# A two-sequence encoder layer: norms of the next sequence, operands of the MLP's first group and the filling at the ends of branch B put in another order

## The chip, the cores and the metric

The kernel runs on one core of a Trainium2 chip. The metric is the device time of one launch, in microseconds (us); lower is better. Engines are named as the profile does: PE (matrix multiply), DVE (vector), ACT (scalar, activation), POOL (general), SP (here it only issues DMAs).

## The reference

One layer of an encoder, all in float32, over two inputs with the same weights: `x_sample` (1 x 512 x 1024) and `x_prompt` (1 x 1024 x 1024).

```python
D_MODEL, HEAD_DIM, D_FF, GRID_W = 1024, 64, 4096, 64

def _token_mixer(xn, w_in, ...):
    z = xn @ w_in
    qa, ka, va, qb, kb, vb, ga, gb = jnp.split(z, idx, axis=-1)
    ...
    o_a = _gqa_attention(qa, ka, va)            # 8 heads, 2 key/value heads
    o_b = _neighbourhood_attention(qb, kb, vb, rpb)   # 8 heads, window 8 x 16 on the token grid
    merged = jax.nn.sigmoid(ga) * (o_a @ w_proj_a) + jax.nn.sigmoid(gb) * (o_b @ w_proj_b)
    return merged @ w_out

def _trunk(x, ...):
    h = x + _token_mixer(_rmsnorm(x, norm_mix_g[l]), ...)
    hn = _rmsnorm(h, norm_mlp_g[l])
    h = h + jnp.square(jax.nn.relu(hn @ w_mlp_up[l])) @ w_mlp_down[l]
    return _rmsnorm(h, norm_final_g)
```

## The kernel before

Every matrix product of float32 operands is made of three passes: each operand is cut into a high part (`hi`, written by ACT, L180 or L1253) and a remainder (`lo`, by DVE, L186 or L1254), and `mm3` (L190) issues hi x hi, lo x hi and hi x lo, which the profile shows as L191, L192 and L193. So each operand of PE passes over ACT and then DVE, and mostly comes from a DMA that SP issues.

The token mixer runs twice (`run`, a "trunk" each), first over `x_sample` (512 tokens, `NB` = 1 block of 512) and then over `x_prompt` (1024 tokens, `NB` = 2). A trunk has these stretches: norm and transposes of x into `xs` (`norm_tile` L249, `transpose_tile` L271, whose PSUM tile is `ptx`), the projection `zs`, branch A, branch B and the merge with the output projection ("phase G"). The MLP then runs over all 1536 tokens in two blocks of 768.

**Branch B** goes through units of one head and one group of 128-query blocks: n = 16 units in the first sequence, 32 in the second. A unit passes three steps, each one unit behind the one before: scores on PE (`sbs`, L930, from `kBs` and `qBs`) with the exponentials, transposes of the probabilities (`ptbs`, L955 and L961, copied to `bhs`), and the product with the values (`obs`, L987). The result of the two last heads goes ACT (`ot_B`), DVE (`os_B`, L994), POOL (L1007), ACT (L1014) and DVE (L1015) into `oX3`, the last of the four operands of the merge. Between the steps PE is given other products, "filling": generators in `fill`, of which `fill.pull(k)` takes k pieces (a piece is one `mm3` of 512 columns). Near the end the filling is `proj_a`, which computes `o_a @ w_proj_a` (`ppas`, 32 pieces in the first sequence), and before it the gate products (`gpss`). How many pieces a unit gets is the number `f` (L1031 to L1034). `proj_a` loads the last part of branch A's output (`rawos`, split into `oXs`) when it is started.

**Phase G** computes `o_b @ w_proj_b` per 128 output columns c (`ppbs`, four `mm3` each, k = 0 to 3, the last from `oX3`), merges, and then computes `merged @ w_out` in two halves of the columns, tile by tile of 128 tokens (`ops`, 24 matmuls each). In the second half of the first sequence, per tile, it also loads a tile of the next sequence's x (`xas`), norms it (`xnns`) and transposes it (`ptxs`), and norms its own output for the MLP (`xnhs`). Loads of the next sequence's first weights (`rawqs`, `rawkvs`, `raw_vs`) come from the pool `rawp`, which has three buffers of 512 KB, tag "raw".

**The MLP** multiplies 2 x 2 blocks with seven products in place of eight. The seven right operands `B_0` to `B_6` are made of transposed tiles by `pair_t` (L310): b11, b21, b12, b22 are four PSUM banks of transposes (`pt`), a1 to a4 sums of them. `pair_t` is called in phase G of the second sequence for three pairs of tiles. The seven left operands `A_0` to `A_6` of a group of 256 columns of `w_mlp_up` are made by `up_steps`, sums `S_0` to `S_3` first where one is needed; the group before carries these steps as "side steps". `up` issues the products into the banks `ua` to `ud`: 12 matmuls of 384 columns each.

The order on each engine is not that of the program text: a scheduler in the build orders all instructions from the data dependences and its own costs, apart from those that `keep_in_program_order` (or `pin=True`) holds in place. Each engine works through its own queue in order.

Of the kernel before, what the change touches and what calls it, by code (L numbers as in the profile page):

```python
# [18 lines left out]
P = 128  # L19
# [42 lines left out]
def encoder(ctx: ExitStack, tc: tile.TileContext, xs, outs, w):  # L62
# [247 lines left out]
    def pair_t(nm, j, tiles, B, banks, tmp):  # L310
# [23 lines left out]
        nc.vector.tensor_tensor(a1, y1, b11, op=ALU.subtract)  # L334
        nc.vector.tensor_tensor(a2, b22, a1, op=ALU.subtract)
        hi(1, a2)
        hi(2, a1)
        nc.vector.tensor_tensor(a3, b22, y1, op=ALU.subtract)
        hi(3, a3)
        nc.vector.tensor_tensor(a4, b21, a2, op=ALU.subtract)  # L340
        hi(4, b22)
        hi(5, b21)
        hi(6, a4)
        lo(4, b22)
        lo(5, b21)
        lo(1, a2)
        lo(2, a1, nc.gpsimd)
        lo(3, a3)
        lo(6, a4, nc.gpsimd)
# [45 lines left out]
    def run(tr, nxt, first):  # L395
# [428 lines left out]
        with phase(f"phB{N}") as ph:  # L824
# [205 lines left out]
            for i in range(n + LS + LV):  # L1030
                if NB == 1:  # L1031
                    f = 9 if i < 1 else 5 if i < n - 4 else 7
                else:
                    f = 5 + (i % 3 > 0) if i < n - 8 else 7  # L1034
# [21 lines left out]
                if i == n - (6 if first else 8):  # L1056
                    pa = proj_a(ph)
                    next(pa)
# [13 lines left out]
        with phase(f"phG{N}") as ph:  # L1072
# [25 lines left out]
            for c in range(NC8):  # L1098
                wp = wp_b.pop(0)
                for c_ in {0: (1, 2), NC8 - 2: (), NC8 - 1: ()}.get(c, (c + 2,)):  # L1100
                    wp_b.append(load_cols(w["w_proj_b"][0], c_ * P, P, f"pb{N}_{c_}", pool_wp))
                for tb in range(NB):
# [5 lines left out]
                    sg = tmp_zs(f"zs{nm}")  # L1108
                    nc.sync.dma_start(sg, zg[1][c * P : (c + 1) * P, tb * 512 : tb * 512 + 512])
                    p_ = mm(f"ppb{nm}")  # L1110
                    for k in range(4):
                        mv = [
                            oX[k][:, i, :].rearrange("p (j r c) -> p r j c", j=4, c=16)[:, tb * 8 : tb * 8 + 8, :, :]
                            for i in range(2)
                        ]
                        mm3(p_, wp[k][0], wp[k][1], mv[0], mv[1], k == 0, k == 3)
# [19 lines left out]
            ahead = []  # L1136

            for half in range(2):
                wo = wos[half]
                hc = slice(half * 512, half * 512 + 512)  # L1140
                for tt in range(NT):
# [15 lines left out]
                    if half == 1 and nxt is not None:  # L1157
                        xt = ph.tile([P, D], F32, tag="k4", name=f"xa{nm}", bufs=4)
                        nc.sync.dma_start(xt, nxt.x[tt * P : (tt + 1) * P, :])
                        ahead.append((tt, norm_tile(xt, gn, ph, f"n{nm}", "k4", 4)))  # L1160
# [68 lines left out]
    def mlp():  # L1229
# [68 lines left out]
        def up_steps(st, ops):  # L1298
# [26 lines left out]
            return [lambda i=i: one(i) for i in (0, 1, 2, 3, 4, 6, 5)]  # L1325
# [7 lines left out]
        def up(st, A, B, side):  # L1333
# [32 lines left out]
            def put(f, half, src, in1=None):  # L1366
# [9 lines left out]
                if f == 0:  # L1376
# [15 lines left out]
            prod(a, 5, 5, True)  # L1392
            put(0, 0, a)
# [108 lines left out]
        def run_up(b, A, B, last):  # L1502

            for fb in range(NFB):
# [5 lines left out]
                up((b, fb), A, B, spread(side, 7))  # L1510
# [265 lines left out]
```

## Time and profile before

| | |
|---|---|
| time, median of 3 runs | 2152.71 us (2152.17 to 2154.12) |
| the profiled execution, own time | 2152.51 us |
| its span in the profile | 2150.7 us |
| granted PE clock, mean | 0.997 |
| DVE, ACT, POOL busy | 69%, 52%, 18% |
| HBM | 264.85 MB read, 87.88 MB written, 164 GB/s over the span |

Places in the span: branch B of the first sequence ends near 310 us and that of the second near 1060; the second half of phase G of the first sequence lies from 356 to 382; the three `pair_t` of phase G from 1184 to 1209; the MLP begins near 1210.

How to read a row of the timeline: start, duration, engine, line, operation, output<-input with shapes, count; in brackets the engine's idle time ahead of the row and what released it. PE's matmuls overlap, so the distance between two starts is what one costs, not its duration. Rows that stand in the prediction aren't shown here.

### The profile page before, as it was taken

Reading aid. Unit: us, or ns where it says so; the run is one execution under the profiler, and the core shown is the slowest. Engines: PE = TensorE matmul, PEld = TensorE weight load, DVE = VectorE, ACT = ScalarE, POOL = GpSimd, SP = SyncE. Lnnn points to the kernel's source line nnn. Section 1 sums busy time; section 2 is a strip of 40 time slices with the busy share of each in tenths; the row PEclk is TensorE's granted clock in tenths of the full one; section 3 lists DMA queues with packets and bytes.
Section 4 is the critical chain, followed back from the end, with each engine's and each line's share of the span. In section 5 each row is a group of like instructions: output and inputs, shape, how many; then the busy total and the mean of one; then the engine's idle time right before and its main releaser. Section 6 shows DMA issues by size and latency. Waiting matters only on the chain. (4 is left out here: it accounts for less than half of the span.)

```text
span 2150.7 us, 31785 instructions
## 1 busy us (share of the span) xinstructions
PE 2120.9 (99%) x10970; PEld 1849.3 (86%) x10970; DVE 1476.2 (69%) x2801; ACT 1115.5 (52%) x2343; POOL 395.3 (18%) x506
## 2 busy tenths in 40 slices
PE   9999999999999999999999999999999999999998
PEld 8887878888898888887888899999999988888886
DVE  6675686677657754656781877778777777759563
ACT  5665554556636644555540566566655643434352
POOL 2232420432243214433300200003000000000000
PEclk9999999999999999999999999999999999999999
DMA  6435557520122132433462655568444799688561
GB/s 195 127 106 163 166 171 256 171 75 25 49 79 75 43 98 86 125 107 102 146 222 106 213 191 180 184 233 222 149 156 154 250 354 338 217 273 282 174 201 63
DMA packets 319578, 350.91 MB, mean 163 GB/s; under 512 B 31160, under 2 KB 255032, under 8 KB 319417
## 3 DMA queue, kind: packets, MB, share of 16 engines
q1 hardware_dynamic: 277927, 279.65, 41.2%
q10 hardware_dynamic: 35810, 52.19, 7.0%
q0 software_dynamic: 5680, 17.04, 2.8%
q8 instruction: 87, 1.43, 0.3%
q14 instruction: 74, 0.61, 0.1%
HBM read 264.85 MB, written 87.88 MB: 164 GB/s over the span
## 5 line engine op out<-in xcount | busy, mean ns | idle before, releaser
L193 PE MATMUL dn<-wd,al 128*128 128x512 f32 x624 | 242.8, 389 | 0.0
L192 PE MATMUL dn<-wd,ah 128*128 128x512 f32 x624 | 242.8, 389 | 0.0
L191 PE MATMUL dn<-wd,ah 128*128 128x512 f32 x624 | 242.7, 389 | 0.0
L1253 ACT ACTIVATE ah<-ar 128x512 fp32r<-128x512 f32 x168 | 104.2, 628 | 199.8 <-PE dn L192 188.6
L1254 DVE TENSOR_TENSOR al<-ar,ah 128x512 fp32r<-128x512 f32 x168 | 115.8, 696 | 76.9 <-ACT ah L1253 65.7
L191 PEld LDWEIGHTS dn<-wd,ah 128*128 128x128 f32 x624 | 117.1, 188 | 24.4
L192 PEld LDWEIGHTS dn<-wd,ah 128*128 128x128 f32 x624 | 117.1, 188 | 24.3
L193 PEld LDWEIGHTS dn<-wd,al 128*128 128x128 f32 x624 | 117.1, 188 | 24.2
L724 POOL TENSOR_SCALAR ps<-ps,rls 128x1024 f32<-128x1024 f32 (+1 forms) x96 | 96.8, 1010 | 215.5 <-DVE rls L723 202.6
L764 DVE TENSOR_TENSOR ptls<-pTs,pths 128x512 fp32r<-128x512 f32 x160 | 107.7, 687 | 37.9 <-ACT pths L763 37.1
L763 ACT ACTIVATE pths<-pTs 128x512 fp32r<-128x512 f32 x160 | 94.2, 598 | 73.8 <-PE pTs L758 71.4
L718 DVE TENSOR_REDUCE nms<-ss 128x1 f32<-128x1024 f32 (+1 forms) x96 | 99.9, 1041 | 25.4 <-PE ss L716 24.9
L176 POOL TENSOR_TENSOR rs_f<-ms_f,mhalf 128x1 f32<-128x1 f32 x6 | 4.0, 667 | 590.7 <-DVE ms_f L172 590.7
L721 ACT ACTIVATE ps<-ss,nms 128x1024 f32<-128x1024 f32 (+1 forms) x96 | 93.3, 973 | 22.5 <-DVE nms L718 20.0
L191 PE MATMUL gpss<-xs_0h,w_gs 128*128 128x512 f32 x256 | 104.7, 409 | 0.3
L758 PEld LDWEIGHTS pTs<-ident,ps 128*128 128x128 f32 x640 | 78.1, 140 | 28.2 <-POOL ps L724 4.3
L193 PE MATMUL gpss<-xs_0h,w_gs 128*128 128x512 f32 x256 | 100.9, 394 | 0.0
L192 PE MATMUL gpss<-xs_0l,w_gs 128*128 128x512 f32 x256 | 100.8, 394 | 0.0
L758 PE MATMUL pTs<-ident,ps 128*128 128x128 f32 x640 | 98.9, 274 | 1.3 <-DVE ptls L764 0.6
L1253 ACT ACTIVATE A<-S 128x512 fp32r<-128x512 f32 x128 | 75.9, 623 | 30.8 <-DVE S L1316 23.5
L1254 DVE TENSOR_TENSOR A<-S,A 128x512 fp32r<-128x512 f32 x128 | 84.5, 686 | 3.9 <-ACT A L1253 3.9
L191 PE MATMUL ud<-B,A 128*128 128x384 f32 x256 | 85.7, 335 | 1.5 <-DVE c L1371 1.5
(325 smaller groups left out, 6380.0 us busy)
## 6 DMA issues: line engine op xcount, KB each, us to landing
ar<-ud SPq DMA_DIRECT2D x120, 512.0 KB
br<-in_w_mlp_down_dram SPq DMA_DIRECT2D x72, 512.0 KB
rawu<-in_w_mlp_up_dram SPq DMA_DIRECT2D x64, 512.0 KB
ud<-c ACTq DMA_DIRECT2D x128, 192.0 KB
raw_gs<-in_w_in_dram SPq DMA_DIRECT2D x32, 512.0 KB
zgs<-sgs ACTq DMA_DIRECT2D x48, 256.0 KB
ud<-cs SPq DMA_DIRECT2D x64, 192.0 KB
raw_os<-in_w_out_dram SPq DMA_DIRECT2D x16, 512.0 KB
```

The lines of the kernel that those rows point to most:

```text
L176: nc.gpsimd.tensor_tensor(r[:, :n], m[:, :n], mhalf[:, :n], op=ALU.pow)
L191: nc.tensor.matmul(out, ah, bh, start=start, stop=False, **kw)
L192: nc.tensor.matmul(out, ah, bl, start=False, stop=False, **kw)
L193: nc.tensor.matmul(out, al, bh, start=False, stop=stop, **kw)
L718: nc.vector.tensor_reduce(nm_, s, axis=AX.X, op=ALU.max, negate=True)
L721: nc.scalar.activation(p, s, AF.Exp, bias=nm_, accum_out=l)
L724: nc.gpsimd.tensor_scalar(p, p, rl, 1.0, op0=ALU.mult, op1=ALU.mult)
L758: nc.tensor.transpose(pt[:, j * P : (j + 1) * P], PP[u, j][:, kc * P : (kc + 1) * P], ident)
L763: nc.scalar.activation(hi, pt, AF.Copy)
L764: nc.vector.tensor_tensor(lo, pt, hi.bitcast(F32), op=ALU.subtract)
L1253: nc.scalar.activation(hi, src, AF.Copy)
L1254: nc.vector.tensor_tensor(lo, src, hi.bitcast(F32), op=ALU.subtract)
```

## The change

Five orders are changed; PE computes the same products.

1. `pair_t`: `B_4`'s high part is copied earlier, and the low parts that read PSUM (`B_4`, `B_5`) come ahead of those that read sums (`B_1`, `B_3`); POOL's two low parts are asked for earlier.
2. Filling of branch B: in the first sequence, the last four units get 6 pieces in place of 7, and the two steps after the last unit 4 and 2. In the second sequence `proj_a` starts a unit earlier (n-9) and the unit n-10 gets no filling.
3. Phase G, c = 0, second sequence: the two products with k = 3 come after the six others.
4. Second half of phase G, first sequence: the four `xas` loads are issued at the first tile, two of them into `rawp`; a tile's norm is issued one tile ahead and its steps, like the `hs` sums, are held in order.
5. MLP, first group of the first block: `A_5`, which is no sum, is made first, and its product is the second, in a bank of its own (`ue`), added to `ua` on DVE.

```diff
@@ -332,21 +332,21 @@
         nc.scalar.activation(y1, b12, AF.Copy)
         lo(0, b11)
         nc.vector.tensor_tensor(a1, y1, b11, op=ALU.subtract)
+        hi(4, b22)
+        hi(2, a1)
         nc.vector.tensor_tensor(a2, b22, a1, op=ALU.subtract)
-        hi(1, a2)
-        hi(2, a1)
+        lo(2, a1, nc.gpsimd)
+        nc.vector.tensor_tensor(a4, b21, a2, op=ALU.subtract)
+        hi(5, b21)
         nc.vector.tensor_tensor(a3, b22, y1, op=ALU.subtract)
-        hi(3, a3)
-        nc.vector.tensor_tensor(a4, b21, a2, op=ALU.subtract)
-        hi(4, b22)
-        hi(5, b21)
         hi(6, a4)
         lo(4, b22)
+        lo(6, a4, nc.gpsimd)
         lo(5, b21)
+        hi(1, a2)
+        hi(3, a3)
         lo(1, a2)
-        lo(2, a1, nc.gpsimd)
         lo(3, a3)
-        lo(6, a4, nc.gpsimd)
...
@@ filling of branch B @@
-                    f = 9 if i < 1 else 5 if i < n - 4 else 7
+                    f = 9 if i < 1 else 5 if i < n - 4 else 6 if i < n else 4 if i == n else 2
                 else:
-                    f = 5 + (i % 3 > 0) if i < n - 8 else 7
+                    f = 0 if i == n - 10 else 5 + (i % 3 > 0) if i < n - 8 else 7
...
-                if i == n - (6 if first else 8):
+                if i == n - (6 if first else 9):
                     pa = proj_a(ph)
...
@@ phase G @@
+                todo = [(tb, k) for tb in range(NB) for k in range(4)]
+                if c == 0:
+                    todo.sort(key=lambda e: e[1] == 3)
+                for tb, k in todo:
...
@@ second half of phase G @@
-                    if half == 1 and nxt is not None:
-                        xt = ph.tile([P, D], F32, tag="k4", name=f"xa{nm}", bufs=4)
-                        nc.sync.dma_start(xt, nxt.x[tt * P : (tt + 1) * P, :])
-                        ahead.append((tt, norm_tile(xt, gn, ph, f"n{nm}", "k4", 4)))
+                    if half == 1 and nxt is not None and tt == 0:
+                        for t_ in (0, 1, 2, 3):
+                            if t_ < 2:
+                                xa[t_] = ph.tile([P, D], F32, tag="k4", name=f"xa{N}_{t_}", bufs=4)
+                            else:
+                                xa[t_] = rawp.tile([P, D], F32, tag="raw", name=f"xa{N}_{t_}")
+                            nc.sync.dma_start(xa[t_], nxt.x[t_ * P : (t_ + 1) * P, :])
+                        ahead.append((0, norm_tile(xa[0], gn, ph, f"n{N}_0", "k4", 4)))
...
-                    while ahead:
+                    if half == 1 and nxt is not None and tt + 1 < NT:
+                        ahead.append((tt + 1, norm_tile(xa[tt + 1], gn, ph, f"n{N}_{tt + 1}", "k4", 4, True)))
+                    if half == 1 and ahead:
                         nxt.p0_t(*ahead.pop(0))
                     if ht is not None:
-                        nc.vector.tensor_tensor(ht[:, hc], o, xr, op=ALU.add)
+                        op = nc.vector.tensor_tensor(ht[:, hc], o, xr, op=ALU.add)
+                        if half == 1 and nxt is not None:
+                            tc.keep_in_program_order(op)
...
@@ MLP @@
-            return [lambda i=i: one(i) for i in (0, 1, 2, 3, 4, 6, 5)]
+            return [lambda i=i: one(i) for i in ((0, 5, 1, 2, 3, 4, 6) if st == (0, 0) else (0, 1, 2, 3, 4, 6, 5))]
...
             prod(a, 0, 0, False)
             nc.scalar.activation(s1, a, AF.Copy)
+            if st == (0, 0):
+                e = bank(f"ue{nm}")[:, 0:HB]
+                prod(e, 5, 5, False)
+                put(0, 0, e, s1)
             prod(bk, 1, 1, False)
...
-            prod(a, 5, 5, True)
-            put(0, 0, a)
+            if st != (0, 0):
+                prod(a, 5, 5, True)
+                put(0, 0, a)
...
-                up((b, fb), A, B, spread(side, 7))
+                if (b, fb) == (0, 0):
+                    side = [[], []] + spread(side, 5)
+                else:
+                    side = spread(side, 7)
+                up((b, fb), A, B, side)
```

What stands on PE at the end of branch B of the first sequence, before (`ppas_7_0` is the last filling, `obs_7_1` and `obs_7_0` the last two units of head 7, `ppbs_0_0` the first merge product, `oXs_1_k` its operand k):

```order
L191 MATMUL ppas_7_0_3735<-oXs_0_3_3251,w_pas_7_3689 128x512
L192 MATMUL ppas_7_0_3735<-oXs_0_3_3251,w_pas_7_3689 128x512
L193 MATMUL ppas_7_0_3735<-oXs_0_3_3251,w_pas_7_3689 128x512
L987 MATMUL obs_7_1_3751<-bhs_7_1_3669,vss_7_3402 128x256 x4
L987 MATMUL obs_7_0_3763<-bhs_7_0_3721,vss_7_3402 128x256 x4
L191 MATMUL ppbs_0_0_3813<-oXs_1_0_3781,w_pbs_0_3731 128x512
L192 MATMUL ppbs_0_0_3813<-oXs_1_0_3781,w_pbs_0_3731 128x512
```

and now:

```order
L193 MATMUL ppas_6_0_3713<-oXs_0_2_3245,w_pas_6_3667 128x512
L987 MATMUL obs_7_0_3737<-bhs_7_0_3695,vss_7_3402 128x256 x4
L191 MATMUL ppas_6_0_3713<-oXs_0_3_3251,w_pas_6_3667 128x512
L192 MATMUL ppas_6_0_3713<-oXs_0_3_3251,w_pas_6_3667 128x512
L193 MATMUL ppas_6_0_3713<-oXs_0_3_3251,w_pas_6_3667 128x512
L191 MATMUL ppas_7_0_3759<-oXs_0_0_3233,w_pas_7_3709 128x512
L192 MATMUL ppas_7_0_3759<-oXs_0_0_3233,w_pas_7_3709 128x512
...
L191 MATMUL ppas_7_0_3759<-oXs_0_3_3251,w_pas_7_3709 128x512
L192 MATMUL ppas_7_0_3759<-oXs_0_3_3251,w_pas_7_3709 128x512
L193 MATMUL ppas_7_0_3759<-oXs_0_3_3251,w_pas_7_3709 128x512
L191 MATMUL ppbs_0_0_3813<-oXs_1_0_3781,w_pbs_0_3755 128x512
L192 MATMUL ppbs_0_0_3813<-oXs_1_0_3781,w_pbs_0_3755 128x512
```

The two `obs` no longer stand together: six `ppas` matmuls are between them, and fifteen between the last `obs` and the first `ppbs` (the first five and the last three of them are shown).

SP's queue in the second half of phase G of the first sequence, before (`xas_1_t` is the next sequence's tile t, `xrs_1_t` a tile of this sequence's x, `raw_os` weights of the output projection, the other `raw` tiles the next sequence's first weights):

```order
L1159 DMA xas_1_0_4161<-in_x_prompt_dram 128x1024
L1152 DMA xrs_1_1_4224<-in_x_sample_dram 128x512
L216 DMA raw_os_1_6_4145<-in_w_out_dram 128x2x512
L448 DMA rawqs_0_0_4425<-in_w_in_dram 128x4x256
L1152 DMA xrs_1_2_4285<-in_x_sample_dram 128x512
L1152 DMA xrs_1_3_4346<-in_x_sample_dram 128x512
L448 DMA rawqs_0_1_4429<-in_w_in_dram 128x4x256
L463 DMA rawkvs_0_4437<-in_w_in_dram 128x8x64 x2
L1159 DMA xas_1_1_4226<-in_x_prompt_dram 128x1024
L216 DMA raw_vs_0_0_4446<-in_w_in_dram 128x4x256
L216 DMA raw_vs_0_4_4451<-in_w_in_dram 128x4x256
L1159 DMA xas_1_2_4287<-in_x_prompt_dram 128x1024
```

and now (`xas_t` is tile t):

```order
L1170 DMA xas_0_4161<-in_x_prompt_dram 128x1024
L1170 DMA xas_1_4163<-in_x_prompt_dram 128x1024
L216 DMA raw_os_1_6_4145<-in_w_out_dram 128x2x512
L1159 DMA xrs_1_1_4238<-in_x_sample_dram 128x512
L1170 DMA xas_2_4165<-in_x_prompt_dram 128x1024
L1159 DMA xrs_1_2_4297<-in_x_sample_dram 128x512
L1159 DMA xrs_1_3_4356<-in_x_sample_dram 128x512
L1170 DMA xas_3_4167<-in_x_prompt_dram 128x1024
L448 DMA rawqs_0_0_4425<-in_w_in_dram 128x4x256
L448 DMA rawqs_0_1_4429<-in_w_in_dram 128x4x256
L463 DMA rawkvs_0_4437<-in_w_in_dram 128x8x64 x2
L216 DMA raw_vs_0_0_4446<-in_w_in_dram 128x4x256
```

`xas_1`, which stood behind five weight loads, now directly follows `xas_0`, and `xas_2` and `xas_3` stand ahead of all weights of the next sequence. On PE the transposes `ptxs_1`, `ptxs_2` and `ptxs_3` stand now after the products of tiles 1, 2 and 3, and before stood near the ends of tile 2, tile 3 and inside the first `zs`.

ACT at the beginning of the MLP, before (`A_0_i` is left operand i of the first group, `A_1_i` of the second, `s_0_0` the two copies of a product bank that later sums need; each `A` row is followed on DVE by its remainder):

```order
L1253 ACTIVATE A_0_1_13126<-S_0_0_13128 128x512
L1253 ACTIVATE A_0_2_13135<-S_0_0_13127 128x512
L1253 ACTIVATE A_0_3_13138<-S_0_0_13129 128x512
L1253 ACTIVATE A_0_4_13142<-S_0_0_13130 128x512
L1253 ACTIVATE A_0_6_13146<-rawu_0_1_13120 128x512
L1253 ACTIVATE A_0_5_13149<-rawu_0_1_13120 128x512
L1253 ACTIVATE A_1_0_13175<-rawu_1_0_13122 128x512
L1380 ACTIVATE s_0_0_13160<-ua_0_13156 128x384
L1384 ACTIVATE s_0_0_13161<-uc_0_13158 128x384
L1253 ACTIVATE A_1_1_13191<-S_0_1_13193 128x512
```

and now:

```order
L1268 ACTIVATE A_0_5_13126<-rawu_0_1_13120 128x512
L1268 ACTIVATE A_0_1_13129<-S_0_0_13131 128x512
L1268 ACTIVATE A_0_2_13138<-S_0_0_13130 128x512
L1268 ACTIVATE A_0_3_13141<-S_0_0_13132 128x512
L1268 ACTIVATE A_0_4_13145<-S_0_0_13133 128x512
L1268 ACTIVATE A_0_6_13149<-rawu_0_1_13120 128x512
L1395 ACTIVATE s_0_0_13160<-ua_0_13156 128x384
L1268 ACTIVATE A_1_0_13206<-rawu_1_0_13122 128x512
L1387 ACTIVATE c_0_0_13189<-c_0_0_13189 128x384
L1388 ACTIVATE c_0_0_13189<-c_0_0_13189 128x384
L1389 DMA ud_0_0_13090<-c_0_0_13189 128x384
```

`A_0_5` moved from sixth to first, and `A_1_0`, an operand of the next group, from ahead of the copy `s_0_0` to behind it. On PE the product of `A_0_5` stands second, and the first twelve matmuls of the next group (`ua_1`) are spread between the last three products of the first.

More of the change, by code (lines that the diff above doesn't have):

```diff
@@ L1101, in run @@
                     wp_b.append(load_cols(w["w_proj_b"][0], c_ * P, P, f"pb{N}_{c_}", pool_wp))
+                zs_of, pp_of = {}, {}
                 for tb in range(NB):
@@ L1107, in run @@
                     nm = f"{N}_{c}_{tb}"
[L1108 to L1116, printed above, removed]
+                    zs_of[tb] = tmp_zs(f"zs{nm}")
+                    nc.sync.dma_start(zs_of[tb], zg[1][c * P : (c + 1) * P, tb * 512 : tb * 512 + 512])
+                    pp_of[tb] = mm(f"ppb{nm}")
+                todo = [(tb, k) for tb in range(NB) for k in range(4)]
+                if c == 0:
+                    todo.sort(key=lambda e: e[1] == 3)
+                for tb, k in todo:
+                    mv = [
+                        oX[k][:, i, :].rearrange("p (j r c) -> p r j c", j=4, c=16)[:, tb * 8 : tb * 8 + 8, :, :]
+                        for i in range(2)
+                    ]
+                    mm3(pp_of[tb], wp[k][0], wp[k][1], mv[0], mv[1], k == 0, k == 3)
+                    if k < 3:
+                        continue
+                    sg, p_ = zs_of[tb], pp_of[tb]
                     nc.vector.scalar_tensor_tensor(sg, sg, 1.0, p_, op0=ALU.add, op1=ALU.mult)
@@ L1135, in run @@
                 gn = gn[:, 0]
-            ahead = []
+            ahead, xa = [], {}
             for half in range(2):
@@ L1375, in put @@
                 kept[f, half] = t
-                if f == 0:
+                if (1 - f, half) in kept:
                     late.append(lambda: total(half))
```

## The prediction

> **What bounds the kernel now.** I read the page's first part, then PE's list of waits, then the timeline of all engines at each wait.
>
> ```profile
> span 2150.7 us, 31785 instructions
> PE 2120.9 (99%) x10970; PEld 1849.3 (86%) x10970; DVE 1476.2 (69%) x2801; ACT 1115.5 (52%) x2343; POOL 395.3 (18%) x506
> ```
>
> PE is busy 2120.9 of 2150.7 us. The change takes no matmul away, so it can win only from the 29.8 us in which PE stands and from stretches in which it runs slowly. The list of PE's waits says which of that the change can reach:
>
> ```profile
> PE ptxs L275 <- DVE xnns L259: 3.0, 3, 2.2
> PE ppbs L191 <- ACT oXs L1014: 2.1, 2, 1.8
> PE ud L191 <- DVE c L1371: 1.5, 1, 1.5
> PE ppas L192 <- DVE oXs L186: 1.2, 1, 1.2
> PE sbs L930 <- DVE kBs L892: 0.8, 1, 0.8
> PE pt L315 <- DVE B L327: 0.8, 1, 0.8
> PE ub L191 <- ACT A L1253: 0.7, 1, 0.7
> ```
>
> Columns: total, times, longest. The seven rows hold 10.1 us, and each one lies where an edit falls. Two of the waits cost more than they last, which the windows show (PE's busy time, then the granted clock, then the DMA share):
>
> ```profile
> 313.50:316.90 3.40, 3.40 (x9) 0.50 0.52 169
> ...
> 388.60:392.00 3.40, 3.40 (x13) 0.50 1.00 337
> ```
>
> About a microsecond after each of the two longest waits (they end at 312.50 and 387.40, in the rows of parts 1 and 3) the clock is 0.50 for 3.4 us. So I count three sorts of loss: the gap, the slow matmul behind it, and the half clock.
>
> **Part 1, filling kept for the end of branch B, first sequence.** All engines there, then PE's next matmuls:
>
> ```profile
> 309.66 0.59 ACT L992 ACTIVATE ot_Bs<-obs 64x512 f32<-64x512 f32 x1 [0.81 <-DVE os_Bs L994]
> 310.12 0.39 PE L192 MATMUL ppbs<-oXs,w_pbs 128*128 128x512 f32 x1
> 310.28 0.68 DVE L994 TENSOR_TENSOR os_Bs<-obs,ot_Bs 64x512 f32<-64x512 f32 x1 [0.72 <-ACT ot_Bs L992]
> 310.34 0.39 PE L193 MATMUL ppbs<-oXs,w_pbs 128*128 128x512 f32 x1
> 311.05 0.96 POOL L1007 TENSOR_TENSOR os_Bs<-os_Bs 64x256 f32<-64x256 f32 x1 [0.61 <-DVE os_Bs L994]
> 312.04 0.41 ACT L1014 ACTIVATE oXs<-os_Bs 64x256 fp32r<-64x256 f32 x1 [1.15 <-POOL os_Bs L1007]
> 312.50 0.50 PE L191 MATMUL ppbs<-oXs,w_pbs 128*128 128x512 f32 x1 [1.77 <-ACT oXs L1014]
> ...
> 313.98 0.63 PE L192 MATMUL ppbs<-oXs,w_pbs 128*128 128x512 f32 x1
> 314.40 0.63 PE L193 MATMUL ppbs<-oXs,w_pbs 128*128 128x512 f32 x1
> ```
>
> Matmuls of 512 columns start 0.23 us apart (310.12, 310.34) and 0.42 us apart at half clock (313.98, 314.40). From 310.34 to 312.50 are 2.16 us, 1.93 over the step. The next two steps are some 0.3 over. In 3.4 us of half clock eight matmuls pass that need 8 x 0.23 = 1.84, so 1.5 are lost. Together **3.7 us**. The chain is ACT, DVE, POOL, ACT: from 309.66 to 312.50, 2.84 us. What covers it after the last `obs` is nine `ppbs` products, 9 x 0.23 = 2.1 us, and the two last `obs` stand side by side, so that ACT's second copy waits 0.81 us for the first one's DVE step. After the change fifteen `ppas` matmuls stand ahead of the nine: 24 x 0.23 = 5.5 us against a chain of 2.9 (4.0 if the 0.81 and a slow POOL step stay). I take 0 left, so gain 3.7. Its price: the units before have six or fewer fill products between them where there were seven, 0.7 us less cover each. The steps before a unit's transposes take 2 to 3 us by these durations, and the shortest new interval is 3.2 us. Bounds: 2 (half the gap comes back upstream, no half clock) to 3.7.
>
> **Part 2, the same in the second sequence.** There one `proj_a` starts a unit earlier, one unit gets no fill, and the last `rawos` is split earlier:
>
> ```profile
> 1005.44 1.38 DVE L892 TENSOR_TENSOR kBs<-pkbs,kBs 64x512 fp32r<-64x512 f32 x2 [0.75 <-ACT kBs L890]
> ...
> 1013.11 1.05 ACT L180 ACTIVATE oXs<-rawos 128x1024 fp32r<-128x1024 f32 x1
> 1014.19 2.60 DVE L186 TENSOR_TENSOR oXs<-rawos,oXs 128x512 fp32r<-128x512 f32 x2 [0.16 <-ACT oXs L180]
> ```
>
> `oXs` at 1014.19 is read at once by `ppas`: the 1.2 us wait of the list, 1.37 with the slow matmul. One of its two DVE steps took 1.9 us, since 0.69 is the step's usual time (1.38 for two). Split a unit earlier, it is off the path: 0. The eight `gpss` matmuls (8 x 0.23 = 1.8 us) now stand between the last `pkbs` and its `sbs`, where PE waited 0.8 (0.95 with the step). But `kBs` now stands behind the two `oXs` steps on DVE (1.38 us), so I leave 0.3. Gain 0.65 + 1.37 = **2.0**; bounds 0 (the two DVE steps are slow there as well, 2.6) to 2.3. Part 2b, `ppbs` with both last thirds at the end: the second `ppbs` wait in the list, 2.1 - 1.8 = 0.3, with its slow matmul **0.5**; nine more matmuls (2 us) cover it.
>
> **Part 3, norms one tile further ahead.**
>
> ```profile
> 349.81 2.96 ACT L180 ACTIVATE wh_os<-raw_os 128x1024 fp32r<-128x1024 f32 x3 [1.50 <-DMA raw_os<-in_w_out_dram]
> ...
> 356.51 0.73 PE L275 MATMUL ptxs<-ident,xnns 128*128 128x128 f32 x5
> ...
> 371.00 0.45 SPq L1159 DMA_DIRECT2D xas<-in_x_prompt_dram  x1
> ...
> 377.22 1.06 ACT L253 ACTIVATE xnns<-xas 128x1024 f32<-128x1024 f32 x1 [1.89 <-DMA xas<-in_x_prompt_dram]
> ...
> 380.16 0.34 SPq L1159 DMA_DIRECT2D xas<-in_x_prompt_dram  x1
> 383.94 1.06 ACT L253 ACTIVATE xnns<-xas 128x1024 f32<-128x1024 f32 x1 [4.53 <-DMA xas<-in_x_prompt_dram]
> 384.70 0.33 PE L191 MATMUL zs<-wghs,xs_0h 128*128 128x384 f32 x1
> 384.87 0.34 PE L192 MATMUL zs<-wgls,xs_0h 128*128 128x384 f32 x1
> 385.97 1.28 DVE L259 SCALAR_TENSOR_TENSOR xnns<-xas,rs_ns,gns 128x1024 f32<-128x1024 f32 x1 [0.69 <-POOL rs_ns L176]
> 387.40 1.06 PE L275 MATMUL ptxs<-ident,xnns 128*128 128x128 f32 x8 [2.19 <-DVE xnns L259]
> 389.33 0.52 PE L191 MATMUL zs<-wghs,xs_0h 128*128 128x384 f32 x1
> 389.65 0.52 PE L192 MATMUL zs<-wgls,xs_0h 128*128 128x384 f32 x1
> ```
>
> The load issued at 380.16 lands at 383.94; the norm then takes 3.3 us (383.94 to 387.25), and PE waits. The three waits are 3.0 us by the list, 3.5 with the slow matmuls behind them. At half clock a 384-column matmul takes 0.32 in place of 0.17: ten in 3.4 us, so 1.5 lost. Together 5.0. Afterwards all four loads are issued in tile 0, and a norm has one tile's 24 matmuls and eight transposes, 24 x 0.23 + 0.9 = 6.4 us, against its 3.3 and what is ahead of it on ACT and DVE (`xs` copies and an `xnhs` norm, up to 3). By this sum the second norm comes about 2 us early and the last one about on time. I leave 0.5: gain **4.5**; bounds 1 (the last one waits over 1.5 us and half clock follows) and 5. What is moved with it: two of the loads now sit in the `raw` buffers, so `rawkvs` of the next sequence waits for the norm of tile 2 and goes out near 372.6, not before 360, and the second `rawqs` some 10 us later. That is the second rival. On SP's queue a second 512 KB load now stands ahead of the last `raw_os`. Before, ACT had split that one by 352.8, and tile 0 (begun just ahead of its transposes at 356.51) reads it after 18 matmuls, so near 361: 8 us of slack, cost 0. The `hs` sums held in order are read by no PE step: 0.
>
> [...]
>
> **Part 4, the MLP's first blocks.**
>
> ```profile
> 1190.43 2.38 DVE L327 TENSOR_TENSOR B<-ta,B 128x512 fp32r<-128x512 f32 x2
> 1192.74 1.27 DVE L327 TENSOR_TENSOR B<-pt,B 128x512 fp32r<-128x512 f32 x2
> ...
> 1213.03 2.20 ACT L1253 ACTIVATE A<-S 128x512 fp32r<-128x512 f32 x4 [5.40 <-PE ua L193]
> 1216.57 1.68 ACT L1253 ACTIVATE A<-rawu 128x512 fp32r<-128x512 f32 x3 [1.35 <-issue]
> ...
> 1223.72 0.55 DVE L1371 TENSOR_TENSOR c<-ud,s 128x384 f32<-128x384 f32 x1
> ```
>
> `pair_t`: the second pair's transposes waited 0.8 for DVE's last read of PSUM, which stood behind two steps on SBUF (2.38 us, one of them 1.7). Ahead of them it ends 2.4 us earlier: **0.9** with the slow matmul, all of it. `ub` waited 0.7 (with what follows 1.3) for the first sum on ACT at 1213.03; a product of twelve 384-column matmuls, 12 x 0.174 = 2.1 us, whose operand is no sum, now stands ahead: **1.3**. `ud` waited 1.5 (1.6) for `c`, which waits for a copy on ACT behind three `A` at 1216.57 to 1218.15. The copy comes 0.5 to 1 us sooner after the last of fewer `A`, and ten matmuls of the next group (1.7 us) are put in between, but the order 2, 3, 4, 6 leaves `uc` and `ud` as close as before to `s` and `c`, and DVE has one more sum (0.55). I leave 0.9: gain **0.7**. Bounds of the three: 1.5 to 3.8. In the MLP's second block `pair_t` is reordered too; PE's list names no wait there, and other products stand between its transposes: 0.
>
> **Sum.** 3.7 + 2.0 + 0.5 + 4.5 + 0.9 + 1.3 + 0.7 = 13.6. For waits that show up nearby and that I can't name I take off 1: of the parts, the second and third are nearest to one. Against the profiled execution, 2152.51 us (span 2150.7 and 1.8 around it, 0.2 under the median of 2152.71): 2152.5 - 12.6 = **2140**.
>
> **The rivals.**
> 1. Part of it comes back: the last norm and the next sequence's weights are late, `kBs` and `uc` wait again. The lower bounds are 2 + 0 + 0.5 + 1 + 1.5 = 5, so 2147.5; typical 2145. For it: part 3 has no margin at its last norm. Against: each place has 2 to 3 us of new cover.
> 2. Slower than before: `rawkvs`, issued near 372.6, must land and be split before `zs` at about 381.7. Loads here took 6.2 us (371.00 to 377.22) and 3.8 us to their first reader, and the split takes under 2: done near 380.6 at the latest, a margin of 1. It turns into a wait from a landing of 7.3 us on, and half clock behind it costs 1.5. To be slower by 0.2% it must take all 12.6 and 4.3 more, so a landing 15 us later: 2157. The DMA share of 1.00 at 388.60 shows that queues can be full.
> 3. No change: the waits move but sum up the same, as PE's list would show under other names: 2151. Or the gaps don't set the clock and the half clock stays: 2140 + 3 = 2143. Against it: both stretches follow the two longest waits. [...]
>
> **How the numbers follow.** All parts within their values, 2136.5 to 2143: 0.52. Rival 1, 2143 to 2148: 0.26. Half clock stays, near 2143: 0.05. No change by 0.2%, which is 4.3 us, about what a measurement can tell here: 0.13. Rival 2: 0.04. Faster 0.83, same 0.13, slower 0.04. Low end: all bounds at their best, 3.7 + 2.3 + 0.5 + 5 + 3.8 = 15.3, so 2137, and 1 for small waits elsewhere: 2136. High end 2148, leaving 0.17 out.
>
> **What would show it.** PE's list without `ppbs` from `oXs`, `ptxs` from `xnns`, `ppas` from `oXs` and `pt` from `B`; clock 1.00 in the windows near 313 and 388; `ud` and `sbs` with under 1 us each. Wrong if a new row above 1 us stands there: `zs` waiting for `wghs` above all, `ptbs` in the units before the end of branch B, or a half-clock stretch elsewhere.

## The result and the profile after

| | us |
|---|---|
| before, median of 6 runs | 2153.56 (2152.17 to 2154.4) |
| changed, median of 6 runs | 2143.10 (2142.86 to 2143.44) |
| ratio | 0.9952, 95% interval 0.9939 to 0.9965 |
| profiled execution, before and after | 2152.51 and 2143.44 |

The change gains 10.5 us by the medians and 9.1 by the two profiled executions, where 12.6 were forecast (2140; the range 2136 to 2148 holds the time). The profile's first part after:

```profile
span 2141.7 us, 31786 instructions
PE 2116.6 (99%) x10970; PEld 1848.3 (86%) x10970; DVE 1469.3 (69%) x2802; ACT 1115.4 (52%) x2343; POOL 393.4 (18%) x506
```

PE stood 29.8 us before and stands 25.1 now. Of its busy time 4.3 us went as well; the two half-clock stretches of before, which the profile after doesn't have, are about 3 of them by the prediction's 1.5 each, and the rest isn't broken down here. PE's list of waits after (total, times, longest):

```profile
PE zs L193 <- DVE xs_1l L291: 2.5, 2, 1.5
...
PE pqs L568 <- DVE rrs L679: 1.2, 1, 1.2
PE sbs L930 <- DVE kBs L892: 1.1, 2, 0.7
...
PE ptxs L275 <- DVE hs L1199: 0.6, 1, 0.6
...
PE ppas L191 <- DVE kBs L892: 0.4, 1, 0.4
...
PE ptbs L955 <- POOL pbs L940: 0.4, 1, 0.4
...
PE uc L191 <- ACT s L1403: 0.2, 1, 0.2
```

The first of these rows in the list of before:

```profile
PE zs L193 <- DVE xs_1l L291: 0.5, 1, 0.5
```

`ppbs` from `oXs`, `ptxs` from `xnns`, `ppas` from `oXs`, `pt`, `ub` and `ud` are gone, all that the change aimed at but one: `sbs` waits for `kBs` still. The wait of `zs` for `xs_1l` grew from 0.5 to 2.5 us and that of `pqs` for `rrs` is new, 3.2 us more in two rows that the prediction had no term for. By stages, first before, then after (window, its length, PE's busy time, granted clock, DMA share; length less busy is PE's idle time; the stages end at other times after the change, so the windows do too, and before the change PE has no idle time from 350 to 365 us):

```profile
300.00:317.00 17.00, 15.23 (x67) 0.90 0.59 186
365.00:393.00 28.00, 25.01 (x123) 0.94 0.81 273
393.00:440.00 47.00, 45.08 (x308) 1.00 0.34 107
1000.00:1030.00 30.00, 27.95 (x137) 1.00 0.45 137
1185.00:1230.00 45.00, 41.95 (x220) 1.00 0.65 213
```

```profile
300.00:317.00 17.00, 17.00 (x83) 1.00 0.71 207
350.00:390.00 40.00, 39.39 (x203) 1.00 0.69 224
390.00:436.00 46.00, 41.66 (x287) 1.00 0.41 126
995.00:1026.00 31.00, 29.42 (x149) 1.00 0.58 176
1180.00:1226.00 46.00, 45.68 (x246) 1.00 0.68 219
```

| stage | PE idle before | after | part |
|---|---|---|---|
| end of branch B, first sequence | 1.8, clock 0.90 | 0 | 1 |
| norms ahead | 3.0, clock 0.94 | 0.6 | 3 |
| first projections of the second sequence | 1.9 | 4.3 | none |
| end of branch B, second sequence | 2.0 | 1.6 | 2 |
| pair_t and first MLP group | 3.0 | 0.3 | 4 |

Two rows differ from the forecast: the projections (row 3) lose 2.4 us more, and the end of the second branch B (row 4) wins 0.5 in place of 2.0. The experiments ask why.

### The profile page after: what moved, and what is told of

Same layout as the page of the kernel before. It is cut to its first block, busy times and chain, and to the rows that moved or that the text cites. A ratio compares the mean times of both kernels' runs of the same rounds, so it can differ in the third digit from the quotient of the medians.

```text
span 2141.7 us, 31786 instructions
## 1 busy us (share of the span) xinstructions
PE 2116.6 (99%) x10970; PEld 1848.3 (86%) x10970; DVE 1469.3 (69%) x2802; ACT 1115.4 (52%) x2343; POOL 393.4 (18%) x506
## 4 chain that ended last, share of the span: by engine, by line
PE 50%; DVE 1%; issue 0%; ACT 0%; DMA 0%; POOL 0%; POOLq 0%; DVEq 0%; ACTq 0%
PE dn L191 6%; PE dn L193 6%; PE dn L192 6%; PE uc L191 2%; PE ud L192 2%; PE uc L192 2%; PE ud L191 2%; PE ud L193 2%; PE uc L193 2%; PE ua L193 2%; PE ua L192 2%; PE ua L191 2%; PE ops L191 1%; PE ops L192 1%; PE ops L193 1%; PE ub L192 1%
## 5 line engine op out<-in xcount | busy, mean ns | idle before, releaser
L1269 DVE TENSOR_TENSOR al<-ar,ah 128x512 fp32r<-128x512 f32 x168 | 115.0, 692 | 71.0 <-ACT ah L1268 63.2
L1387 ACT ACTIVATE c<-c 128x384 f32<-128x384 f32 x97 | 50.7, 524 | 68.1 <-DVE c L1386 68.1
```

The costliest lines, as they stand in the source:

```text
L1269: nc.vector.tensor_tensor(lo, src, hi.bitcast(F32), op=ALU.subtract)
L1387: nc.scalar.activation(t, t, AF.Relu)
```

## The experiments

All are the changed kernel with one edit. Medians stand against the changed kernel's 2143.10 unless another is named. The runs are from several chips: the kernel before took 2153.56 us beside the changed kernel, 2154.21 beside undo_norm, the other undo runs, xt_swap and pa10, 2152.46 beside hs_free and hs_free_swap and 2152.75 beside the last pair. So a difference of less than about 1 us between two chips' medians shows nothing, and what a part is worth is read at its place in the trace (the table of stretches in the next section).

**undo_norm**: part 3 undone.

```diff
-                    if half == 1 and nxt is not None and tt == 0:
-                        for t_ in (0, 1, 2, 3):
...
+                    if half == 1 and nxt is not None:
+                        xt = ph.tile([P, D], F32, tag="k4", name=f"xa{nm}", bufs=4)
...
+                        ahead.append((tt, norm_tile(xt, gn, ph, f"n{nm}", "k4", 4)))
```

> The changed kernel with part 3 undone: loads, norms and hs sums of the second half of phase G stand as before. Theory (part 3 saves 5.0 us at the norms and gives 2.2 us back in the next sequence's projections and 0.8 at its first transposes, because the load of tile 4 now waits for the store of the last xnhs): 2.0 us slower than the changed kernel, about 2145.1; the list shows ptxs waiting for xnns again (3.0 us in all), one half-clock stretch behind the longest of these waits, and PE's losses between 390 and 440 us fall from 5.1 to about 2.9 us. Rival (all of the 5.0 lasts, and the new waits in the projections belong to part 1, which lets PE arrive earlier): 5.0 us slower, about 2148, and the waits in the projections stay at 5 us.

Measured: 2145.24 (2144.20 to 2145.98, five runs), 2.1 us slower, where the theory has 2.0. PE's list has the three waits back and the projections' waits small:

```profile
PE ptxs L275 <- DVE xnns L259: 3.5, 3, 2.2
PE ptxs L275 <- DVE xns L378: 1.3, 4, 0.6
...
PE pqs L568 <- DVE rrs L679: 0.7, 1, 0.7
PE zs L193 <- DVE xs_1l L291: 0.5, 1, 0.5
```

So part 3 brings the new waits in the projections; part 1, still in this kernel, doesn't. The clock did another thing than expected. The gap of 2.2 us at the third norm has no half clock behind it, and three short waits near 280 us, which the changed kernel has too, do.

```profile
277.10:280.50 3.40, 1.84 (x12) 1.00 0.41 113
280.50:283.90 3.40, 3.40 (x11) 0.50 0.40 129
382.90:386.30 3.40, 1.77 (x11) 1.00 0.38 154
386.30:389.70 3.40, 2.81 (x19) 1.00 0.92 294
```

In that half clock matmuls of 512 columns start 0.43 us apart (281.27, 281.70) and 0.23 ahead of it (276.13, 276.36), so it costs the profiled execution about 1.5 us; it has nothing to do with part 3, and the kernel before takes 0.65 more on this chip, so the agreement with the theory's 2.0 is partly luck. Between the first `ops` and the first `gpss` of the second sequence, which takes in the norms and the projections, PE needs 1.5 us more here than in the changed kernel: that is what part 3 as it was built is worth.

**undo_fill1**: the first sequence's filling as before.

```diff
-                    f = 9 if i < 1 else 5 if i < n - 4 else 6 if i < n else 4 if i == n else 2
+                    f = 9 if i < 1 else 5 if i < n - 4 else 7
```

> The changed kernel with the first sequence's filling as before (7 pieces to the end). Theory (the gap of 1.8 us and the half clock behind it are both due to the missing cover; 3.7 us there, less 0.8 us that the thinner filling costs in the units before): 2.9 us slower, about 2146.0, ppbs waiting about 1.8 us for oXs and a stretch of 3.4 us at clock 0.50 that begins within 1.5 us of the end of that wait. Rival (the half clock has another cause, or the projections take the time back because PE reaches them later): 1.4 us slower or less, about 2144.5, clock 1.00 behind the gap or smaller waits in the projections. [...]

Measured: 2145.05 (2143.72 to 2147.30, five runs), 2.0 us slower, less than the 2.9 of the theory and more than the rival's 1.4. The profiled execution, itself 2145.05, has the wait of `ppbs` at 1.8 us and this behind it:

```profile
310.00:313.40 3.40, 1.63 (x7) 1.00 0.56 183
313.40:316.80 3.40, 3.40 (x10) 0.50 0.45 145
```

The half clock there follows the gap; the waits in the projections were as in the changed kernel. The single times reach over 3.6 us, with six runs of the changed kernel within 0.6, so the median fixes the size badly; from the first `ppbs` to the first `ops` PE needs 3.8 us more here than in the changed kernel, and as long as before the change.

**undo_fill2**: the second sequence's filling as before.

```diff
-                    f = 0 if i == n - 10 else 5 + (i % 3 > 0) if i < n - 8 else 7
+                    f = 5 + (i % 3 > 0) if i < n - 8 else 7
...
-                if i == n - (6 if first else 9):
+                if i == n - (6 if first else 8):
```

> The changed kernel with the second sequence's filling as before (proj_a one unit later, no unit without filling). Theory (the trace after shows 2.1 us of losses left around it: sbs behind kBs 0.8, ppas 0.6, sbs 0.7, against 2.5 before): 0.9 us slower, about 2144.0, ppas waiting 1.2 us for oXs again. The prediction's size: 2.0 us slower, 2145.1. Rival (the two orders cost the same): within 0.3 us.

Measured: 2143.02 (2142.49 to 2143.73, four runs): no difference by the times, as the rival has it. The waits came back as expected:

```profile
PE ppas L192 <- DVE oXs L186: 1.2, 1, 1.2
PE sbs L930 <- DVE kBs L892: 1.0, 2, 0.8
```

At the place the rival isn't borne out: from the last `pqbs` to the first `ppbs` of the second sequence PE needs 95.28 us here, 95.32 before and 94.45 in the changed kernel, so part 2 is worth 0.8 us there, near the theory's 0.9. The profiled execution of undo_fill2 was 1.6 us ahead of the changed one by 450 us, long before the edit; the medians of two chips don't resolve 0.8.

**undo_mlp**: the first MLP group as before.

```diff
-            if st == (0, 0):
-                e = bank(f"ue{nm}")[:, 0:HB]
-                prod(e, 5, 5, False)
-                put(0, 0, e, s1)
...
-            if st != (0, 0):
-                prod(a, 5, 5, True)
-                put(0, 0, a)
+            prod(a, 5, 5, True)
+            put(0, 0, a)
```

> The changed kernel with the first MLP group as before (product 5 last, no bank of its own). Theory (by the traces the first group lost 2.9 us before and 0.35 after): 2.5 us slower, about 2145.6, ub waiting 0.7 us for A and ud 1.5 us for c again. The prediction's size: 2.0 us slower. Rival (the later groups take part of it back, since their operands are ready later too): 1 us slower or less.

Measured: 2145.31 (2144.02 to 2147.97, four runs), 2.2 us slower, near the theory. Its profiled execution is the longest, 2147.97, was granted a mean clock of 0.998 (0.999 in the changed kernel's) and has one longer `pt` wait besides, 1.3 us. At the place itself:

```profile
1209.84 0.45 PE L191 MATMUL ub<-B,A 128*128 128x384 f32 x1 [0.72 <-ACT A L1268]
1219.75 0.44 PE L191 MATMUL ud<-B,A 128*128 128x384 f32 x1 [0.75 <-DVE c L1386]
```

`ub` waits as before the change, `ud` only half as long as the 1.5 expected.

**xt_swap**: the tile of the norm's output allocated ahead of the load's.

```diff
-                    xt = norm_load(x, tr.ready, ph, f"{N}_{tr.ready}")
                     xn_next = ph.tile([P, D], F32, tag="xn", name=f"xn{N}_{tr.ready}", bufs=2)
+                    xt = norm_load(x, tr.ready, ph, f"{N}_{tr.ready}")
```

> The changed kernel with one edit: in the next sequence's first stretch the norm's output tile is allocated ahead of the load's tile, so that the load of tile 4 falls on memory that the last transposes free and no longer on that of the last xnhs, whose store it waits for. Theory (that wait delays the projections): the load of tile 4 is issued near 382 us in place of 390.3, PE's losses between 390 and 440 us fall from 5.1 to 3 us or less, and the kernel is 2 us faster than the changed one, about 2141. Rival (the stretch is paced by its own chain of norm, transposes, split and projection, some 8.7 us a tile, whenever it begins): the load is early, the losses stay within 0.5 us of 5.1, 2143.

Measured: 2142.72 (2142.15 to 2142.81, five runs), 0.4 us faster; the rival. The load goes out 9 us earlier, at 381.29 and not 390.26, and PE waits where it did:

```profile
381.29 0.65 SPq L246 DMA_DIRECT2D xts<-in_x_prompt_dram  x1
```

```profile
403.18 1.09 PE L275 MATMUL ptxs<-ident,xns 128*128 128x128 f32 x8 [0.38 <-DVE xns L378]
408.09 0.44 PE L193 MATMUL zs<-wghs,xs_1l 128*128 128x384 f32 x1 [1.50 <-DVE xs_1l L291]
```

My theory on the load fell. Set beside the same two rows of before and of the changed kernel, the trace shows what it is:

```profile
407.44 1.10 PE L275 MATMUL ptxs<-ident,xns 128*128 128x128 f32 x8 [0.28 <-DVE xns L378]
...
412.38 0.44 PE L193 MATMUL zs<-wghs,xs_1l 128*128 128x384 f32 x1 [0.53 <-DVE xs_1l L291]
```

```profile
403.94 1.09 PE L275 MATMUL ptxs<-ident,xns 128*128 128x128 f32 x8 [0.38 <-DVE xns L378]
408.87 0.44 PE L193 MATMUL zs<-wghs,xs_1l 128*128 128x384 f32 x1 [1.50 <-DVE xs_1l L291]
```

From the transposes to the projection that reads them PE takes 4.94 us before and 4.93 after, both times until the split by ACT and DVE is done (DVE's `xs_1l`, 0.68 us long, begins at 411.64 before and at 408.13 after); 0.53 of that is waiting before and 1.50 after. There is less other work between the two. The built order says so (first rows of each block on PE, tile 4's transposes `ptxs_4`, its reader `zs_0_4`), before and then after:

```
1837 L191 MATMUL zvs_0_1_4719<-wvs_0_4419,xs_0h_4196 128x256
1839 L275 MATMUL ptxs_4_4670<-ident,xns_4_4418 128x128 x8
1840 L193 MATMUL zvs_0_1_4719<-wvs_0_4419,xs_0l_4198 128x256
1863 L191 MATMUL zs_0_4_4809<-wghs_0_0_4423,xs_1h_4666 128x384
```

```
1839 L191 MATMUL zvs_0_1_4719<-wvs_0_4419,xs_0h_4210 128x256
1852 L275 MATMUL ptxs_4_4670<-ident,xns_4_4418 128x128 x8
1853 L192 MATMUL zvs_0_1_4719<-wvs_1_4420,xs_0h_4211 128x256
1865 L191 MATMUL zs_0_4_4809<-wghs_0_0_4423,xs_1h_4666 128x384
```

In the trace 22 `zvs` and three `pqs` matmuls stand between the transposes and their first reader before, 11 `zvs` and three `pqs` after. No line of the change names these instructions; the scheduler put them so.

**pa10**: `proj_a` of the second sequence another unit earlier.

```diff
-                    f = 0 if i == n - 10 else 5 + (i % 3 > 0) if i < n - 8 else 7
+                    f = 0 if i == n - 11 else 5 + (i % 3 > 0) if i < n - 8 else 7
...
-                if i == n - (6 if first else 9):
+                if i == n - (6 if first else 10):
```

> The changed kernel with proj_a of the second sequence another unit earlier (n-10, and no filling at n-11), so that all splits of oXs stand ahead of the last kBs on ACT and DVE by a unit. Theory (the losses left there, sbs waiting for kBs 0.65 and ppas 0.4 behind it, come from the oXs steps that stand directly ahead of kBs on DVE, 2.64 us for four): these two waits go, 1 us faster, about 2142.1. Rival (pkbs ends too late for its sbs whatever stands ahead of kBs): sbs waits for kBs as now, within 0.3 us.

Measured: 2144.55 (2143.69 to 2144.87, four runs), 1.4 us slower. `sbs` waits as the rival has it. In the changed kernel the `oXs` steps do stand ahead of `kBs`:

```profile
997.57 2.64 DVE L186 TENSOR_TENSOR oXs<-rawos,oXs 128x512 fp32r<-128x512 f32 x4
997.82 1.06 ACT L180 ACTIVATE oXs<-rawos 128x1024 fp32r<-128x1024 f32 x1 [1.93 <-DMA rawos<-oads]
998.91 1.20 ACT L890 ACTIVATE kBs<-pkbs 64x512 fp32r<-64x512 f32 x2
1000.22 1.38 DVE L892 TENSOR_TENSOR kBs<-pkbs,kBs 64x512 fp32r<-64x512 f32 x2
...
1001.66 0.63 PE L930 MATMUL sbs<-kBs,qBs 128*128 128x384 f32 x2 [0.65 <-DVE kBs L892]
```

In pa10 nothing stands ahead of them, and PE waits no less:

```profile
1003.87 0.62 PE L930 MATMUL sbs<-kBs,qBs 128*128 128x384 f32 x2 [0.79 <-DVE kBs L892]
```

because the unit without filling moved too and took PE's cover away: eight `gpss` matmuls stand between the last `pkbs` and this `sbs` in the changed kernel, none in pa10. The two splits of `kBs` take 2.7 us in a row (998.91 to 1001.60) with the `oXs` steps and 2.6 without them (1001.20 to 1003.81); what decides is how much PE has to do meanwhile.

**undo_pair** and **undo_ppb**, one execution each: `pair_t` in the old order, and without the sort by k.

```diff
+        hi(1, a2)
+        hi(2, a1)
...
-        lo(4, b22)
-        lo(6, a4, nc.gpsimd)
-        lo(5, b21)
...
```

```diff
-                if c == 0:
-                    todo.sort(key=lambda e: e[1] == 3)
```

> The changed kernel with pair_t in the old order. Theory: the second pair's transposes wait about 0.76 us for DVE's B again and the later one's 0.3 goes, 0.6 us slower, about 2143.7; one look can't tell that in the time, the list of waits can. Rival (the earlier place of the transposes on PE did it, not the order on DVE): no wait of pt above 0.3 us.

> The changed kernel with the two k = 3 products of phase G's first column block in the old places. Theory: ppbs waits about 0.4 us for oXs near 1070 us and loses 0.55 us there, 2143.6. Rival (the earlier end of branch B has moved that chain ahead too): no such wait, 2143.1.

Measured: 2143.80 and 2144.44, single times that tell nothing of parts this small; the lists of waits do. First undo_pair, then undo_ppb:

```profile
PE pt L315 <- DVE B L327: 0.8, 1, 0.8
```

```profile
PE ppbs L191 <- ACT oXs L1014: 0.4, 1, 0.4
```

Both theories hold: each wait is back at its old place and near its old size, and PE needs 0.7 us more at each place. The list of undo_pair has one row more, which neither theory nor rival named: `uc` waits 1.4 us for `s` in the MLP's first group, and 0.2 in the changed kernel. So the order in `pair_t` may be worth more than its own wait; one execution doesn't settle it.

**hs_free** and **hs_free_swap**: part 3 without one piece, the `hs` sums held in order; the second with the edit of xt_swap too.

```diff
                         op = nc.vector.tensor_tensor(ht[:, hc], o, xr, op=ALU.add)
-                        if half == 1 and nxt is not None:
-                            tc.keep_in_program_order(op)
```

> The changed kernel without one piece of part 3: the hs sums of phase G's second half are no longer held in order; loads and norms stand as changed. In the built order this brings the transposes of tile 4 (ptxs_4) and the first pqs back ahead: ptxs_4 then has 4 zs, 24 zvs and 3 pqs matmuls between it and the projection that reads it, against 11 zvs, 3 pqs and 2 zs in the changed kernel (22 zvs, 3 pqs and 2 zs before the change). Theory (the 5.3 us of losses between 390 and 440 us, against 2.9 before, come from that order on PE): the wait of zs for xs_1l (1.5 us) and that of pqs for rrs (1.2 us) shrink to 0.5 or go, losses 3 us or less, 2 us faster than the changed kernel, about 2141. Rival (the norm of tile 4 on DVE at 402.6 us is what is late, so transposes asked for earlier only wait themselves): ptxs waits 1.5 us or more for xns, the sum of the losses stays at 5, 2143.

> As hs_free, and the load of tile 4 on memory that comes free early (the edit of xt_swap). Theory (with the order mended the load becomes what is late, so its 8 us earlier issue counts now): another 0.5 to 1 us faster than hs_free, about 2140.3, ptxs waiting under 0.3 us for xns. Rival (the norm's place on DVE and not the load sets it): same as hs_free within 0.3 us.

Measured: hs_free 2141.19 (2139.38 to 2143.46, five runs), hs_free_swap 2141.47 (2140.51 to 2142.52, five runs). The theory of hs_free holds, its rival in part: the wait for `xs_1l` and the one for `rrs` left the list, and the transposes wait for the norm more often,

```profile
PE ptxs L275 <- DVE xns L378: 2.1, 4, 1.1
```

but the sum fell. PE now has 5.5 us from tile 4's transposes to the row that waited, and doesn't wait there:

```profile
398.83 1.09 PE L275 MATMUL ptxs<-ident,xns 128*128 128x128 f32 x8 [1.07 <-DVE xns L378]
...
404.30 0.44 PE L193 MATMUL zs<-wghs,xs_1l 128*128 128x384 f32 x1
```

The norms' stage and the projections in its profile:

```profile
350.00:390.00 40.00, 40.00 (x209) 1.00 0.78 259
390.00:436.00 46.00, 43.74 (x306) 1.00 0.32 101
```

The projections stand 2.3 us and not 4.3, and the norms lose nothing without the held sums. The earlier load of hs_free_swap adds nothing: the rival.

**changed_again** and **hs_free_again**: the changed kernel and hs_free on one chip.

> The changed kernel itself, as the reference for the next run on the same chip. [...] Rival (executions differ by the waits themselves): times spread evenly, no half clock in the profile even where the time is long.

> The kernel of hs_free beside the changed one on the same chip. Theory (the hs sums held in order cost 2.2 us in the next sequence's projections by the order that the scheduler then builds): median 2 us below changed_again's, 0.1%. Rival (the 2 us seen so far were the chip's): within 0.5 us.

Measured: changed 2143.32 (2141.98 to 2144.28, five runs), hs_free 2140.97 (2140.00 to 2141.99, five runs): 2.35 us apart, the theory. Against the kernel before on that chip (2152.75) the ratios are 0.9954 (0.9941 to 0.9966) and 0.9946 (0.9932 to 0.9959). These intervals overlap; the single times of the two kernels meet only at their ends (2141.98 and 2141.99). The spread of changed_again isn't shown to come from the half clock: its profiled execution, the longest at 2144.28, was granted a mean clock of 0.999, as the changed kernel's was, 1.00 from 350 to 436 us, and stood 5.3 us in the projections (46.00 less 40.71 in the same window). There the rival fits: those waits vary too.

## Why the prediction came out as it did

What each part gained is read best as the time that PE takes from one row to another around it, since that leaves out what other places of the same execution do. In us, from the profiles (the forecast and the last column are gains):

| from the first row of ... to the first of ... | before | changed | that part undone | forecast | gained |
|---|---|---|---|---|---|
| last run of `pkbs`, first sequence, to `ppbs` | 41.83 | 42.61 | 41.97 (undo_fill1) | part 1: 0 | -0.8 |
| `ppbs` to `ops`, first sequence | 26.04 | 22.20 | 26.04 (undo_fill1) | part 1: 3.7 | 3.8 |
| `ops` to `gpss` of the second sequence | 117.80 | 116.31 | 117.76 (undo_norm) | part 3: 4.5 | 1.5 |
| last run of `pqbs`, second sequence, to `ppbs` | 95.32 | 94.45 | 95.28 (undo_fill2) | part 2: 2.0 | 0.9 |
| `ppbs` to `ops`, second sequence | 45.07 | 44.40 | 45.09 (undo_ppb) | part 2b: 0.5 | 0.7 |
| `pt` to `ua` | 28.08 | 27.40 | 28.08 (undo_pair) | `pair_t`: 0.9 | 0.7 |
| `ua` to the next `pt` | 234.20 | 231.37 | 233.51 (undo_mlp) | `ub`, `ud`: 2.0 | 2.8 |

The stretches add up to 9.6; the changed kernel's execution had lost 0.5 by 31 us, ahead of every edit, and with that it is the 9.1 of the profiled executions.

1. **The bound and the waits** were right: all the gain lay in PE's idle time and its slow stretches, and every wait that the change was to take away went, that for `kBs` in part.
2. **Part 1**, 3.7 forecast: 3.8 came at the place, 1.8 us of idle time and the half clock with it. But its price in the units ahead, put at nothing, was not nothing: `ptbs` waits 0.3 to 0.4 for `pbs` near 287 us in every profile with the new filling and in neither without it (before and undo_fill1). Up to 0.5 more near 277 us, `sbs` behind `kBs`, varies between profiles of the same filling (0 in xt_swap, 0.5 in the changed kernel).
3. **Part 2**, 2.0 forecast, 0.9 gained. The prediction left 0.3 for `kBs` behind two `oXs` steps. Four stand ahead of it, ACT's copy of the last too, and `kBs` came 0.65 late; `ppas` and a later `sbs` wait 0.4 and 0.5 behind it. That stayed within the lower bound (0). Part 2b (0.5) is right.
4. **Part 3, the step that failed most**: 4.5 forecast, 1.5 gained. At the norms themselves it came: 3.0 us idle went to 0.6 in the changed kernel's profile (to 0 in changed_again's and in xt_swap's), with the half clock. What failed is the term "The `hs` sums held in order are read by no PE step: 0". They are read by none, and yet holding them gave PE another order in the next stretch, where 2.4 us came back. Without that piece alone, hs_free, PE takes 112.83 us in the third row of the table (112.87 in hs_free_again), a gain of 5.0; the nine profiles with the new norms and held sums have 115.0 to 116.4. By the medians on one chip the piece costs 2.35. "1 for waits that show up nearby" was the sum's only price for it, and the rival on `rawkvs` named a wrong carrier (in the second sequence `zs` never waits for `wghs`). It could be read beforehand: the built order showed `ptxs_4` eleven rows nearer to its reader, and the trace had the price of a row (two `zvs` start 0.12 us apart).
5. **Part 4**, 2.9 forecast, 3.5 gained. `uc` waits 0.2 in the profile, where 0.9 was left for it and `ud`. How the last row's 2.8 divides isn't clean: undo_mlp keeps 0.7 of it, and undo_pair, with its wait of `uc`, has 232.61 there.
6. **The half clock** was priced as if each long gap brought it. The experiments show that the length of one gap doesn't decide it, as the last section says; the term of 3.0 us for two stretches holds for the profiled execution of before. Other executions of that kernel were granted mean clocks of 0.997 to 0.999. One stretch of 3.4 us at 0.50 in 2151 us takes 0.0008 from the mean, so by this estimate they didn't all have the same number of such stretches.

So the time in the range is right for the reason given in parts 1, 2b and 4. That it came near although parts 2 and 3 fell short by 4.1 us and part 1 had its price of 0.8 is partly luck: part 4 gave 0.6 more than forecast, and the 1 us taken off without a name covered some of the rest.

Which rule of the scheduler moves `ptxs_4` when the `hs` sums are held in order stays open; that it does is shown by hs_free, where only that piece differs, and its 2.35 us by hs_free_again beside changed_again.

## What to carry to other kernels

Where a scheduler sets the order, a change's price isn't only at its place: compare the built order of the stretches behind it too, and for each consumer that waited, count the work between it and its producer. Fixing instructions in order is an edit by itself, with a price of its own; here it cost 2.35 us, more than the second sequence's filling and the order of `pair_t` gained together, and the norms needed none of it. When a wait is removed by moving filling, look where the filling came from.

## What the hardware showed that was not expected

The half clock didn't follow the length of a gap. In the profile of before, each of the two longest waits (1.77 and 2.19 us) had 3.4 us at clock 0.50 about a microsecond behind it, from 313.5 and from 388.6 us, and undo_fill1 has the same behind its wait of 1.8 us, from 313.4. In undo_norm the wait at the third norm is back, from 384.7 to 386.9, and is no shorter:

```profile
386.89 1.06 PE L275 MATMUL ptxs<-ident,xnns 128*128 128x128 f32 x8 [2.22 <-DVE xnns L259]
```

There the clock stayed at 1.00, in the windows from 366 to 438 us. Near 280 us of the same profile three waits of 0.5, 0.4 and 0.7 us had the half clock behind them (1.84 of 3.40 us busy, then 0.50, above). The changed kernel has the same waits, of 0.48, 0.41 and 0.67 us, from 277.1 to 280.0, and its clock stays at 1.00:

```profile
277.80:281.20 3.40, 2.32 (x15) 1.00 0.32 92
281.20:284.60 3.40, 3.40 (x19) 1.00 0.33 100
```

So neither the longest wait nor the waits by themselves tell whether a half clock follows. The idle share of a stretch doesn't decide alone either: in undo_norm PE stood 1.63 of the 3.40 us from 382.9 to 386.3 and the clock stayed at 1.00 in the 3.40 us behind them, and it stood 1.56 of those from 277.1 to 280.5 and the clock behind them was 0.50. What decides it isn't shown by any run here.

Executions of one kernel differ in the granted clock too: of the kernel before, on the chip of hs_free, the three executions with a mean granted clock of 0.999 took 2151.06 to 2153.24 us and the three with 0.997 took 2153.18 to 2154.00.
